# A fused two-block kernel: the last token tile's expert choice moved into the dense stage, other choices two heads at a time, 128-row expert biases

## The chip, the cores and the metric

The kernel runs as one program on one core of a Trainium2 chip. The metric is the device time of one launch in microseconds (us), as the median of several runs. The engines are named as in the profile: PE is TensorE's matmul side and PEld its weight loads, DVE is VectorE, ACT ScalarE, POOL GpSimd, SP SyncE.

## The reference, cut to what matters

Two transformer blocks over 512 tokens of 1024 numbers, all in float32. The first has a mixture of 32 experts with four chosen per token, the second a PEER layer: each of 8 heads picks 16 of 16384 small experts for every token.

```python
def moe_ffn(h, ...):
    top_logits, top_idx = lax.top_k(hf @ router_w + router_b, TOP_K)      # 4 of 32
    gates = jax.nn.softmax(top_logits, axis=-1)
    ...
        gu = xb @ w_gate_up[e] + b_gate_up[e]                             # 1024 -> 2048
        ...
        act = (up + 1.0) * gate * jax.nn.sigmoid(SWIGLU_ALPHA * gate)
        return act @ w_down[e] + b_down[e]                                # 1024 -> 1024
    ...
    out = out.at[tok_sorted].add(y_sorted * gate_sorted[:, None])

def _peer(h, w_query, sub_keys, expert_u, expert_v):
    q = (t @ w_query).reshape(n_tok, P_HEADS, 2, P_DQ)
    sc = jnp.einsum('thcd,hckd->thck', q, sub_keys)                       # 2 x 128 key scores per head
    s1, i1 = lax.top_k(sc[:, :, 0], 16); s2, i2 = lax.top_k(sc[:, :, 1], 16)
    cand = (s1[..., :, None] + s2[..., None, :]).reshape(n_tok, P_HEADS, 256)
    top_s, top_i = lax.top_k(cand, 16)
    experts = take(i1, top_i // 16) * 128 + take(i2, top_i % 16)
    gates = jax.nn.softmax(top_s, axis=-1)
    act = gelu(einsum('td,tkd->tk', t, expert_u[experts])) * gates
    return einsum('tk,tkd->td', act, expert_v[experts])
```

## The kernel before, in words

The program is written in one order; each engine works through its own queue in order when it runs. A planner in the framework chose the order of each queue when the kernel was built: it starts from the program's order as priorities and may put a later instruction ahead of an earlier one that waits. So work that stands late in the program can fill an earlier gap of an engine, as far as its data and its memory are there.

Large float32 products are taken as three products of two halves: `split` writes `hi`, a rounded copy (ACT, L116), and `lo`, the rest (DVE, L117, or POOL where asked), and PE multiplies hi by hi, hi by lo and lo by hi. Weights stream in over SP's queue, are split, and multiplied.

**The expert mixture (MoE).** `moe` (L660) goes over 32 experts of 96 token rows (CB) each. For expert i it issues the gate-up products (`Expert.gate_up`, L602), the next expert's token gather and its transposes (`load_x`, L578, `transpose_split`, L571), the down products of expert i-1 (`down`, L633), and the activation (`swiglu`). At odd i a piece of a side product runs (`ple`, L546 and L548), after i = 1 a piece of `slot_map`. Raw weights have four buffers (`wraw`), the halves three each. Four `gu` and two `dn` accumulators are opened by a bias product: `biases` (L641) lays each bias out as 64 rows, 32 of the rounded value and 32 of the rest; `sel` has for expert i ones in rows i and 32+i, so one matmul of 64 rows adds both halves to every token row (L672):

```python
bias = lambda t: (lambda out, n: nc.tensor.matmul(out, sel[:, i:i + 1].to_broadcast([64, CB]),
                                                  t[:, n * S:(n + 1) * S], start=True, stop=False))
```

There are four of these per expert for gate-up and two for down, 192 in all. The expert outputs are scattered to Y, and later gathered per token and weighted by the gates (`Route.rest`, L451, makes `e.gates`). Blocks beyond 96 rows of an expert go through an overflow loop with a bias of its own.

**The PEER layer**, in `peer` (L2084), has these stages. *Queries* (L1834): 16 half-heads c; the products give scores for 4 tiles of 128 tokens (NT); tiles 0 to 2 are searched at once (`best`, that is `top16`: five DVE operations for the best 16 of a row), and the scores of the last tile are kept in `sc3`. After each odd c the head's choice is made for three tiles (`select`, L1878): `pair_sums` adds 50 candidate pairs in seven small operations on DVE, and their numbers in seven on POOL (`cid`); `top16` for each tile; then `eq`, a mask of 16 x 50 on DVE (L1897), multiplied by `cid` on POOL (L1899), and summed on DVE a step later (`rest`, L1904). *Gates* (L1922): for tiles 0 to 2 the chosen experts become dense 128 x 128 gate tables by one-hot products (`ohA`, `ohB`, `gp`), written to DRAM (`GD`, L1959 to L1961); beside it the first 24 `up` products of the dense stage run (GEB). *The last tile's choice*, L2110 to L2117:

```python
for c in range(16):
    pr.best(pr.sel, pr.sc3[:, c], NT - 1, c)
rest = [pr.select(slice(NT - 1, NT), 0)]
for h in range(1, NH):
    rest.append(pr.select(slice(NT - 1, NT), h))
    rest.pop(0)()
```

*Dense stage*, 128 steps b: `up` streams 128 rows of expert_u for the three tiles (`up`, L1963, `dots`, then Gelu into `ge`, 24 steps ahead until it runs out), `acts` multiplies by the gates read back from `GD` (`gch`, one load for four steps, L1994; `dact` L1997, its halves `dah` and `dal`, L2003 and L2004), `down` adds the products with expert_v to `y` (L2012). Memory of the choice's pool is closed ahead of this stage and given to its tiles, `vhi` among them. Beside it, *gathers* (`gathered`, L2015): the last tile's experts aren't dense; in 144 turns POOL fetches one row of expert_u and one of expert_v per token (`gu`, `gv`, L2022), which DVE uses two turns later (L2032, L2043). A step takes one turn, two where b % 8 is 1 or 5. At b = 114 the gathers have to be through, and the last tile is finished.

The changed places in full:

Of the kernel before, what the change touches and what calls it, by code (L numbers as in the profile page):

```python
# [359 lines left out]
class Route:  # L360
# [90 lines left out]
    def rest(self):  # L451
# [10 lines left out]
        nc.vector.tensor_mul(e.gates, gt, gs.to_broadcast([P, NT, TOPK]))  # L462
        pe = pool.tile([P, NT, NE], F, name="pe")
# [91 lines left out]
class Expert:  # L555


    def __init__(self, e, pools, wgu, wdn, tok, out, bias_gu, bias_dn, nm):
        self.e, self.wgu, self.wdn, self.tok, self.out = e, wgu, wdn, tok, out
        self.bias_gu, self.bias_dn, self.nm = bias_gu, bias_dn, nm  # L560
        self.pw, self.px, self.ps_gu, self.ps_dn, self.ps_t = pools
        self.ahead = []
# [57 lines left out]
    def down(self):  # L620
# [20 lines left out]
def biases(e, pool, raw):  # L641

    nc, a = e.nc, e.a
    e.esel = e.mc.tile([64, NE], R, name="sel")
    for t_, nm in ((e.bg, "b_gate_up"), (e.bd, "b_down")):
        for o in range(0, t_.shape[1], D):
            r = raw([64, D], "braw")
            for h in range(2):
                nc.gpsimd.dma_start(r[32 * h:32 * h + 32, :], a[nm][:, o:o + D])
            t = t_[:, o:o + D]  # L650
            nc.scalar.copy(t, r)
            nc.vector.tensor_sub(t[32:64, :], r[32:64, :], t[32:64, :].bitcast(F))
# [6 lines left out]

def moe(e):  # L660
    nc, tc, a = e.nc, e.tc, e.a
    bg, bd, sel = e.bg, e.bd, e.esel
    with ExitStack() as c2:
# [7 lines left out]
        def make(i):  # L671
            bias = lambda t: (lambda out, n: nc.tensor.matmul(out, sel[:, i:i + 1].to_broadcast([64, CB]),  # L672
# [3 lines left out]
                          e.slot_tok[:, i:i + 1], e.slot_out[:, i:i + 1], bias(bg), bias(bd), str(i))  # L676
# [6 lines left out]
        side, smap = ple(e, px, ps_t), slot_map(e, px)  # L683
        for i, x in enumerate(ex):
# [29 lines left out]
        with tc.For_i(0, n_over, 1) as i:  # L714
# [7 lines left out]
            br2 = px.tile([P, D], F, name="ov_bd", bufs=1)  # L722
            nc.sync.dma_start(br2[0:1, :], a["b_down"][bass.ds(ei, 1), :])
# [6 lines left out]
                       so[:, 1:2], so[:, 0:1], bias(br), bias(br2), "o")  # L730
# [1045 lines left out]
class Peer:  # L1776
# [11 lines left out]
    def open(self, ctx):  # L1788
# [3 lines left out]
        self.s = self.pd.tile([P, NT, NH, 2, NK], F, name="pk_s")  # L1792
        self.ixu = self.pd.tile([P, NT, NH, 2, NK], U32, name="pk_iu")
# [4 lines left out]
        self.ts = self.sel.tile([P, NT, NH, NK], F, name="pk_ts", bufs=1)  # L1798
        self.idf = self.sel.tile([P, NT, NH, NK], F, name="pk_id", bufs=1)
# [34 lines left out]
    def queries(self, pool, ps, ahead):  # L1834
# [14 lines left out]
        for c in range(16):  # L1849
# [25 lines left out]
    def best(self, pool, sc, t, c):  # L1875
        top16(self.e, pool, sc, self.s[:, t, c // 2, c % 2, :], self.ixu[:, t, c // 2, c % 2, :], "a")

    def select(self, tiles, h):  # L1878

        e, nc, pool, s = self.e, self.e.nc, self.sel, self.s  # L1880
        n = tiles.stop - tiles.start
        ixf = pool.tile([P, NT - 1, 2, NK], F, name="pk_if")[:, 0:n]
        nc.vector.tensor_copy(ixf, self.ixu[:, tiles, h])
        cand = pool.tile([P, NT - 1, NC], F, name="cand")[:, 0:n]
        pair_sums(nc.vector, cand, s[:, tiles, h, 0, :], s[:, tiles, h, 1, :])
# [374 lines left out]
```

## Time and profile before

| what | value |
|---|---|
| median of 3 runs | 4267.72 us (4267.01 to 4272.81) |
| profiled execution | 4264.27 us, its span 4262.4 us |
| mean granted TensorE clock | 0.979 of full speed |
| PE, PEld | busy 4069.3 us (95%), 3240.0 us (76%) |
| DVE, ACT, POOL | busy 3162.1 us (74%), 2033.2 us (48%), 1047.8 us (25%) |

The span is the time from the first to the last instruction of the core in one profiled execution; the execution's own time has a little around it. A view of groups gives line, engine, operation, output and inputs by the program's names, shape and count, busy time and the mean of one in ns, and after the last bar the idle time ahead of it with what ended most of it. A timeline row is start, duration, engine, line, operation, shapes and count, and in brackets the idle time before it and its releaser. PEclk is the granted clock in tenths of full speed or as a share.

### The profile page before, as it was taken

The page shows a single profiled execution, that of the slowest core. Times are in us where ns is not written, and L with a number is a line of the kernel's source. Part 1 is how long each engine was busy: PE and PEld are TensorE (multiplying, and loading weights), DVE is VectorE, ACT ScalarE, POOL GpSimd, SP SyncE. Part 2 cuts the span into 40 slices and gives each one's busy share as a digit, 9 for nine tenths or more (in the row PEclk, how much of TensorE's full clock was granted, in tenths as well). Part 3 has the DMA queues.
Part 4 walks back from the last instruction along what each step waited for, and adds up shares of the span by engine and source line. Part 5 has one row for each costly group of instructions (what it writes and reads, how often), then busy time and mean ns, then how long its engine had stood idle before and what let it go on. Part 6 is the DMA issues. An engine that isn't in the chain of part 4 may idle for free. (4 is left out here: it accounts for less than half of the span.)

```text
span 4262.4 us, 60165 instructions
## 1 busy us (share of the span) xinstructions
PE 4069.3 (95%) x22534; PEld 3240.0 (76%) x22534; DVE 3162.1 (74%) x5533; ACT 2033.2 (48%) x2876; POOL 1047.8 (25%) x929
## 2 busy tenths in 40 slices
PE   9999999999999979999999999999896999999998
PEld 7556666666666638877888888777786999999997
DVE  8778888888888875766676666456988577777777
ACT  3356666666666654434444444333385333333333
POOL 5402221220000030110011110015556244344431
PEclk9999999999999989999999999999998999999999
DMA  3679999999999863212321222443155788888884
GB/s 126 212 292 330 334 348 330 335 346 334 338 342 332 333 225 98 73 63 83 95 85 58 77 75 78 148 135 109 65 193 207 263 300 308 311 310 302 304 303 166
DMA packets 355415, 933.84 MB, mean 219 GB/s; under 512 B 60928, under 2 KB 169376, under 8 KB 322224
## 3 DMA queue, kind: packets, MB, share of 16 engines
q1 hardware_dynamic: 299168, 741.19, 49.2%
q0 software_dynamic: 49536, 176.18, 11.2%
q10 hardware_dynamic: 6416, 12.58, 0.9%
q8 instruction: 179, 2.93, 0.3%
q14 instruction: 116, 0.95, 0.1%
HBM read 865.66 MB, written 64.20 MB: 218 GB/s over the span
## 5 line engine op out<-in xcount | busy, mean ns | idle before, releaser
L117 DVE TENSOR_TENSOR wlo<-wraw,whi 128x2048 fp32r<-128x2048 f32 x384 | 873.1, 2291 | 101.9 <-ACT whi L116 101.2
L116 ACT CAST whi<-wraw 128x2048 fp32r<-128x2048 f32 x384 | 721.5, 1909 | 124.6 <-DMA wraw<-in_w_gate_up_dram 88.4
L1972 PE MATMUL dots<-hp_h,ulo 128*128 128x384 f32 x1024 | 351.9, 344 | 15.6 <-POOL ulo L117 15.3
L1972 PE MATMUL dots<-hp_h,uhi 128*128 128x384 f32 x1024 | 352.7, 344 | 2.2 <-ACT uhi L116 2.2
L1972 PE MATMUL dots<-hp_l,uhi 128*128 128x384 f32 x1024 | 351.1, 343 | 0.0
L2022 POOL DMA_INDIRECT gu<-in_expert_u_dram,idx x128 | 193.5, 1512 | 432.3 <-DVE gu L2032 412.8
L602 PE MATMUL gu<-wlo,xhi 128*96 128x512 f32 x1024 | 297.5, 410 | 0.0
L602 PE MATMUL gu<-whi,xhi 128*96 128x512 f32 x1024 | 283.7, 397 | 0.6 <-ACT xhi L116 0.6
L116 ACT CAST uhi<-uraw 128x1024 fp32r<-128x1024 f32 x128 | 134.1, 1048 | 314.6 <-PE dots L1972 232.6
L602 PE MATMUL gu<-whi,xlo 128*96 128x512 f32 x1024 | 280.0, 394 | 0.0
L2012 PE MATMUL y<-vhi,dah 128*128 128x512 f32 x762 | 238.5, 394 | 28.8 <-ACT dah L2003 28.8
L2012 PE MATMUL y<-vhi,dal 128*128 128x512 f32 x762 | 236.3, 391 | 0.0
L2012 PE MATMUL y<-vlo,dah 128*128 128x512 f32 x762 | 235.8, 390 | 0.0
L602 PEld LDWEIGHTS gu<-whi,xhi 128*96 128x96 f32 x1024 | 163.2, 162 | 73.7 <-ACT yx L636 4.4
L602 PEld LDWEIGHTS gu<-whi,xlo 128*96 128x96 f32 x1024 | 165.4, 162 | 70.5
L2004 DVE TENSOR_TENSOR dal<-dact,dah 128x384 fp32r<-128x384 f32 x127 | 71.0, 559 | 197.5 <-ACT dah L2003 197.0
L2003 ACT CAST dah<-dact 128x384 fp32r<-128x384 f32 x127 | 65.1, 513 | 309.8 <-issue 261.1
L602 PEld LDWEIGHTS gu<-wlo,xhi 128*96 128x96 f32 x1024 | 158.8, 162 | 66.4 <-issue 8.9
L1972 PEld LDWEIGHTS dots<-hp_h,ulo 128*128 128x128 f32 x1024 | 194.9, 190 | 17.1 <-POOL ulo L117 16.3
L1972 PEld LDWEIGHTS dots<-hp_h,uhi 128*128 128x128 f32 x1024 | 195.0, 190 | 6.8 <-ACT uhi L116 2.6
L1972 PEld LDWEIGHTS dots<-hp_l,uhi 128*128 128x128 f32 x1024 | 195.1, 191 | 4.1
L578 POOL DMA_INDIRECT xg<-H,slot_tok x32 | 38.7, 1209 | 626.2 <-PE mtp L571 424.8
(720 smaller groups left out, 10397.7 us busy)
## 6 DMA issues: line engine op xcount, KB each, us to landing
wraw<-in_w_gate_up_dram SPq DMA_DIRECT2D x256, 1024.0 KB, 5.8
wraw<-in_w_down_dram SPq DMA_DIRECT2D x128, 1024.0 KB, 7.2
uraw<-in_uT_dram SPq DMA_DIRECT2D x128, 512.0 KB, 5.0
vraw<-in_expert_v_dram SPq DMA_DIRECT2D x128, 512.0 KB, 3.8
wuraw<-in_w2p_dram SPq DMA_DIRECT2D x72, 512.0 KB, 3.2
GD<-gst SPq DMA_DIRECT2D x36, 640.0 KB, 4.9
gch<-GD SPq DMA_DIRECT2D x30, 768.0 KB, 12.1
piece<-in_w_ada_dram SPq DMA_DIRECT2D x24, 512.0 KB, 4.1
```

What stands on the lines that cost most here:

```text
L116: e.copied = e.nc.scalar.copy(hi, src).ins
L117: (eng or e.nc.vector).tensor_sub(lo, src, hi.bitcast(F))
L578: e.gathered = nc.gpsimd.indirect_dma_start(out=xg, out_offset=None, in_=e.H, in_offset=bass.IndirectOffsetOnAxis(ap=self.tok, axis=0)).ins
L602: nc.tensor.matmul(self.gu[n], l[:, k, :], r[:, cs], start=False, stop=k == KD - 1 and r is lo)
L1972: nc.tensor.matmul(dots, l[:, k, :], r[:, k, 0:ND], start=k == 0 and i == 0, stop=k == KD - 1 and i == 2)
L2003: nc.scalar.copy(ah, act)
L2004: self.anchor = nc.vector.tensor_sub(al, act, ah.bitcast(F)).ins
L2012: self.e.nc.tensor.matmul(y[t][:, cs], l[:, t * P:(t + 1) * P], r[:, cs], start=b == 0 and l is ah and r is hi, stop=b == P - 1 and l is al)
L2022: nc.gpsimd.indirect_dma_start(out=g, out_offset=None, in_=src, in_offset=bass.IndirectOffsetOnAxis(ap=idx[:, h, k:k + 1], axis=0))
```

## The change

**Expert biases.** The gate-up bias and `sel` get 128 rows, of which rows 64 to 127 of the bias are zero. The down bias leaves the experts and the overflow loop: `Route.rest` spreads the gates over the 32 experts (`e.gm`), and a new generator `down_bias` transposes them (four transposes, one ACT copy) and adds gates times b_down to `e.xpre` by eight float32 matmuls of 32 rows and eight DVE additions, one after each even expert from i = 2 on.

```diff
+        e.gm = e.mc.tile([P, NT, NE], F, name="gm")
+        go = pool.tile([P, NT, TOPK, NE], F, name="go")
+        nc.vector.tensor_mul(go, oh, e.gates[:, :, :, None].to_broadcast([P, NT, TOPK, NE]))
+        nc.vector.reduce_sum(e.gm, go.rearrange("p t j e -> p t e j"), axis=AX.X)
...
-            self.bias_dn(dn[n], n)
         for k2 in range(4):
...
-    v = pool.tile([64, NE], F, name="selv", bufs=1)
+    e.esel = e.mc.tile([P, NE], R, name="sel")
+    nc.gpsimd.dma_start(e.bd, a["b_down"])
+    for o in range(0, 2 * D, D):
+        r = raw([P, D], "braw")
+        nc.gpsimd.memset(r[64:P, :], 0.0)
+        for h in range(2):
+            nc.gpsimd.dma_start(r[32 * h:32 * h + 32, :], a["b_gate_up"][:, o:o + D])
+        t = e.bg[:, o:o + D]
+        nc.scalar.copy(t, r)
+        nc.vector.tensor_sub(t[32:64, :], r[32:64, :], t[32:64, :].bitcast(F))
+    v = pool.tile([P, NE], F, name="selv", bufs=1)
...
+def down_bias(e, pool, ps):
+
+    nc = e.nc
+    gT = pool.tile([NE, S], F, name="gT", bufs=1)
+    t = ps.tile([P, S], F, name="gTp", tag="plep")[0:NE]
+    for i in range(NT):
+        nc.tensor.transpose(t[:, i * P:(i + 1) * P], e.gm[:, i, :], e.ident)
+    nc.scalar.copy(gT, t)
+    for i in range(NT):
+        for n in range(2):
+            yield
+            cs = slice(n * S, (n + 1) * S)
+            b = ps.tile([P, S], F, name="bdp", tag="plep")
+            nc.tensor.matmul(b, gT[:, i * P:(i + 1) * P], e.bd[:, cs], start=True, stop=True)
+            nc.vector.tensor_add(e.xpre[:, i, cs], e.xpre[:, i, cs], b)
+    yield
+
+
...
-            bias = lambda t: (lambda out, n: nc.tensor.matmul(out, sel[:, i:i + 1].to_broadcast([64, CB]),
+            bias = lambda t: (lambda out, n: nc.tensor.matmul(out, sel[:, i:i + 1].to_broadcast([P, CB]),
                                                               t[:, n * S:(n + 1) * S], start=True, stop=False))
...
             if i % 2 == 1:
                 next(side, None)
+            elif i > 1:
+                next(downs, None)
...
-                e.bg, e.bd = fp.tile([64, 2 * D], R, name="bg"), fp.tile([64, D], R, name="bd")
+                e.bg, e.bd = fp.tile([P, 2 * D], R, name="bg"), fp.tile([NE, D], F, name="bd")
```

**The choice for tiles 0 to 2.** The key scores and indices are kept in one tile for three token tiles and one for the last. `select` takes two heads, so six rows, at c = 3, 7, 11, 15, and the summing of a group follows two half-heads later, at c = 5, 9 and 13, and after the loop. `pairs` and `marked` are helpers shared with the last tile.

```diff
-        self.s = self.pd.tile([P, NT, NH, 2, NK], F, name="pk_s")
-        self.ixu = self.pd.tile([P, NT, NH, 2, NK], U32, name="pk_iu")
+        rows = lambda n, dt, nm: self.pd.tile([P, NH * n, 2, NK], dt, name=nm)
+        self.s, self.ixu = (rows(NT - 1, F, "pk_s"), rows(1, F, "pk_sl")), (rows(NT - 1, U32, "pk_iu"), rows(1, U32, "pk_il"))
...
-            if c % 2:
-                rest.append(self.select(slice(0, NT - 1), c // 2))
-            elif c:
+            if c % 4 == 3:
+                rest.append(self.select(c // 4))
+            elif c % 4 == 1 and c > 4:
                 rest.pop()()
...
+    def pairs(self, pool, last, rs):
...
+        nc.vector.tensor_copy(ixf, ixu[:, rs])
+        cand = pool.tile([P, n, NC], F, name="cand", bufs=1)
+        pair_sums(nc.vector, cand, s[:, rs, 0, :], s[:, rs, 1, :])
+        i1 = pool.tile([P, n, NK], F, name="i1")
         nc.vector.tensor_scalar(i1, ixf[:, :, 0, :], float(P), None, op0=OP.mult)
-        cid = pool.tile([P, NT - 1, NC], F, name="cid")[:, 0:n]
+        cid = pool.tile([P, n, NC], F, name="cid", bufs=1)
         pair_sums(nc.gpsimd, cid, i1, ixf[:, :, 1, :])
-        tu, tf = pool.tile([P, NT - 1, NK], U32, name="tu")[:, 0:n], pool.tile([P, NT - 1, NK], F, name="tf")[:, 0:n]
...
+        return cand, cid, pool.tile([P, n, NK], U32, name="tu"), pool.tile([P, n, NK], F, name="tf")
+
+    def marked(self, eq, io, tf, cid):
+        nc = self.e.nc
+        nc.vector.tensor_tensor(eq, io[:, None, 0:NC].to_broadcast([P, NK, NC]), tf[:, :, None].to_broadcast([P, NK, NC]),
+                                op=OP.is_equal)
+        nc.gpsimd.tensor_mul(eq, eq, cid[:, None, :].to_broadcast([P, NK, NC]))
+        return eq
...
+    def select(self, g):
...
+        e, nc, pool, n = self.e, self.e.nc, self.sel, NT - 1
+        cand, cid, tu, tf = self.pairs(pool, False, slice(2 * n * g, 2 * n * (g + 1)))
+        at = lambda x, r: x[:, r % n, 2 * g + r // n, :]
+        for r in range(2 * n):
+            top16(e, pool, cand[:, r, :], at(self.ts, r), tu[:, r, :], "b")
         nc.vector.tensor_copy(tf, tu)
...
+        eqs = [self.marked(pool.tile([P, NK, NC], F, name="eq", bufs=6), self.io_ps, tf[:, r, :], cid[:, r, :])
+               for r in range(2 * n)]
...
         def rest():
-            for t, eq in enumerate(eqs):
-                nc.vector.reduce_sum(self.idf[:, tiles.start + t, h, :], eq, axis=AX.X)
+            for r, eq in enumerate(eqs):
+                nc.vector.reduce_sum(at(self.idf, r), eq, axis=AX.X)
```

**The last tile's choice** becomes a generator, `late`, with its small tiles in the memory of `yg`, and masks in the gather buffers (`gt`). Eight dense steps take two `top16` rows each, then four groups of two heads take two steps each. The gathers follow at the same one `next` per dense step; the generator stops after two turns of every three, so of two steps one carries one gather turn and the other two.

```diff
+    def late(self, pool):
+
+        e, nc = self.e, self.e.nc
+        room, off, views = self.yg, [0], {}
...
+        ar = Arena()
+        ts, idf = ar.tile([P, NH, NK], F, name="l_ts"), ar.tile([P, NH, NK], F, name="l_id")
+        for c in range(0, 16, 2):
+            for i in range(2):
+                self.best(ar, self.sc3[:, c + i], NT - 1, c + i)
+            yield
+        for g in range(4):
+            cand, cid, tu, tf = self.pairs(ar, True, slice(2 * g, 2 * g + 2))
+            for i in range(2):
+                top16(e, ar, cand[:, i, :], ts[:, 2 * g + i, :], tu[:, i, :], "b")
+            nc.vector.tensor_copy(tf, tu)
+            yield
+            eqs = [self.marked(pool.tile([P, D], F, name="leq", tag="gt", bufs=6)[:, 0:NK * NC].rearrange("p (k c) -> p k c", k=NK),
+                               self.iota, tf[:, i, :], cid[:, i, :]) for i in range(2)]
+            yield
+            for i, eq in enumerate(eqs):
+                nc.vector.reduce_sum(idf[:, 2 * g + i, :], eq, axis=AX.X)
+        self.last_choice = self.chosen(ts, idf, self.pc, ar)
...
-    for c in range(16):
-        pr.best(pr.sel, pr.sc3[:, c], NT - 1, c)
-    rest = [pr.select(slice(NT - 1, NT), 0)]
-    for h in range(1, NH):
-        rest.append(pr.select(slice(NT - 1, NT), h))
-        rest.pop(0)()
-    rest.pop()()
-    idx, gt = pr.chosen(NT - 1, pr.pc)
...
-    gather = pr.gathered(idx, gt, pool)
+
+    def last_tile():
+        yield from pr.late(pool)
+        for i, x in enumerate(pr.gathered(*pr.last_choice, pool)):
+            if i % 3 < 2:
+                yield
+
+    gather = last_tile()
...
-        for _ in range(2 if b % 8 in (1, 5) else 1):
-            next(gather, None)
+        next(gather, None)
```

`chosen` takes its arrays and its pool as arguments, with the same operations as before.

## Rows read from the trace of the kernel before

**Rows 1.** The page's first part: busy time, share of the span, instructions of each engine

```profile
PE 4069.3 (95%) x22534; PEld 3240.0 (76%) x22534; DVE 3162.1 (74%) x5533; ACT 2033.2 (48%) x2876; POOL 1047.8 (25%) x929
```

**Rows 2.** Windows: us, busy PE, PEld, DVE, ACT, POOL (operations), PEclk, DMA, GB/s

```profile
228.00:1520.00 1292.00, 1279.86 (x5632) 867.54 (x5632) 1088.77 (x806) 841.21 (x660) 192.30 (x94) 1.00 0.91 334
...
3040.00:3077.00 37.00, 21.68 (x90) 20.96 (x90) 31.77 (x127) 11.61 (x16) 18.52 (x16) 0.72 0.28 100
3077.00:3258.00 181.00, 169.25 (x1192) 159.00 (x1190) 154.47 (x375) 145.72 (x331) 113.71 (x127) 1.00 0.51 189
3258.00:3287.00 29.00, 0.23 (x2) 0.00 (x0) 27.56 (x70) 6.10 (x8) 18.06 (x37) 0.54 0.34 106
...
3680.00:3810.00 130.00, 130.00 (x654) 118.38 (x654) 98.77 (x122) 45.21 (x63) 54.44 (x40) 1.00 0.85 306
```

**Rows 3.** Timeline of PE around an expert's down bias (start us, us, operation)

```profile
664.72 0.62 PE L602 MATMUL gu<-wlo,xhi 128*96 128x512 f32 x2
665.18 0.49 PE L571 MATMUL mtp<-ident,sw_a 96*128 96x96 f32 x4
...
666.91 1.09 PE L602 MATMUL gu<-whi,xlo 128*96 128x512 f32 x4
667.93 0.46 PE L672 MATMUL dn<-bd,sel 64*96 64x512 f32 x1
668.33 1.18 PE L602 MATMUL gu<-wlo,xhi 128*96 128x512 f32 x4
```

**Rows 4.** Windows, tile sel alone: us, busy PE, PEld, DVE, then as before

```profile
228.00:1520.00 1292.00, 80.23 (x192) 28.17 (x192) 0.00 (x0) 1.00 0.91 334
```

**Rows 5.** Waits of ACT, 400 to 1400 us: total us, times, longest

```profile
ACT whi L116 <- DMA wraw<-in_w_gate_up_dram: 79.9, 46, 4.1
```

**Rows 6.** Windows: ten microseconds of the MoE, columns as in Rows 2

```profile
610.00:620.00 10.00, 10.00 (x43) 6.22 (x41) 9.01 (x9) 3.32 (x4) 0.00 (x0) 1.00 1.05 384
```

**Rows 7.** Timelines of SP, ACT, DVE and PE at the hand-over to the dense stage

```profile
3253.77 1.86 SPq L1961 DMA_DIRECT2D GD<-gst  x3
...
3280.57 1.04 ACT L116 CAST vhi<-vraw 128x1024 fp32r<-128x1024 f32 x1 [3.67 <-POOL eq L1899]
3280.72 1.19 ACTq L1994 DMA_DIRECT2D gch<-GD  x2
...
3285.86 1.03 DVE L1997 TENSOR_TENSOR dact<-ge,gch 128x384 f32<-128x384 f32 x2 [0.61 <-DMA gch<-GD]
...
3287.02 1.22 PE L2012 MATMUL y<-vhi,dah 128*128 128x512 f32 x2 [28.79 <-ACT dah L2003]
```

**Rows 8.** DMA issues: queue, count, KB of one, median us from issue to landing

```profile
GD<-gst SPq DMA_DIRECT2D x36, 640.0 KB, 4.9
```

**Rows 9.** Timeline of DVE in a dense step with two gather turns

```profile
3711.32 0.56 DVE L2004 TENSOR_TENSOR dal<-dact,dah 128x384 fp32r<-128x384 f32 x1 [2.09 <-ACT dah L2003]
...
3715.28 1.22 DVE L2032 SCALAR_TENSOR_TENSOR gu<-gu,hp_g 128x1024 f32<-128x1024 f32 x1
...
3716.42 1.28 DVE L2043 SCALAR_TENSOR_TENSOR yg<-gv,pact,yg 128x1024 f32<-128x1024 f32 x1
...
3719.67 0.56 DVE L2004 TENSOR_TENSOR dal<-dact,dah 128x384 fp32r<-128x384 f32 x1 [0.34 <-ACT dah L2003]
```

**Rows 10.** Tile gu, 3500 to 3900 us: issue ns min/median/max, then landing

```profile
L2022 POOL DMA_INDIRECT gu<-in_expert_u_dram,idx x60: 933/1678/1687, 3504.3 to 3897.2; - x60
...
DMA to landing us min/median/max: 5.6/6.6/9.7
```

**Rows 11.** Timeline of PE: float32 matmuls of 256 columns

```profile
689.51 1.56 PE L546 MATMUL plep<-wg,hT 128*128 128x256 f32 x6
```

**Rows 12.** Timeline of DVE where the routing ends

```profile
203.71 0.19 DVE L418 SCALAR_TENSOR_TENSOR q<-pp,selt 128x32 f32<-128x32 f32 x1 [7.62 <-PE pp L417]
```

**Rows 13.** Groups by form of POOL, 2900 to 3070 us

```profile
L1899 POOL TENSOR_TENSOR eq<-eq,cid 128x800 f32<-128x800 f32 x24 | 41.5, 1756 | 17.0 <-DVE eq L1897 17.0
```

**Rows 14.** Timeline of PE at the end of the queries

```profile
3046.77 0.69 PE L1972 MATMUL dots<-hp_h,ulo 128*128 128x384 f32 x1 [6.71 <-POOL ulo L117]
```

**Rows 15.** Windows, tile pk_s alone: us, DVE busy, PEclk, DMA, GB/s

```profile
3077.00:3258.00 181.00, 27.06 (x135) 1.00 0.51 189
```

More of the change, by code (lines that the diff above doesn't have):

```diff
@@ L633, in down @@
                         nc.tensor.matmul(dn[n], l[:, k, :], r[:, j * D + n * S:j * D + (n + 1) * S],
-                                         start=False, stop=k == KD - 1 and r is lo)
+                                         start=k == 0 and l is ah and r is hi, stop=k == KD - 1 and r is lo)
         for n in range(2):
@@ L643, in biases @@
     nc, a = e.nc, e.a
[L644 to L652, printed above, removed]
-    v = pool.tile([64, NE], F, name="selv", bufs=1)
+    e.esel = e.mc.tile([P, NE], R, name="sel")
[9 more added lines that the diff above has]
+    v = pool.tile([P, NE], F, name="selv", bufs=1)
     nc.gpsimd.iota(v, pattern=[[1, NE]], base=0, channel_multiplier=-1, allow_small_or_imprecise_dtypes=True)
-    v2 = pool.tile([64, NE], F, name="selv2", bufs=1)
+    v2 = pool.tile([P, NE], F, name="selv2", bufs=1)
     nc.vector.tensor_scalar(v2, v, -32.0, None, op0=OP.is_equal)
     nc.vector.scalar_tensor_tensor(e.esel, v, 0.0, v2, op0=OP.is_equal, op1=OP.add)
+def down_bias(e, pool, ps):
[13 more added lines that the diff above has]
+    yield
 def moe(e):
     nc, tc, a = e.nc, e.tc, e.a
-    bg, bd, sel = e.bg, e.bd, e.esel
+    bg, sel = e.bg, e.esel
     with ExitStack() as c2:
@@ L696, in moe @@
         prev.down()
-        for it in (side, smap):
+        for it in (side, smap, downs):
             for _ in it:
@@ L1875, in best @@
     def best(self, pool, sc, t, c):
[L1876 to L1885, printed above, removed]
-        i1 = pool.tile([P, NT - 1, NK], F, name="i1")[:, 0:n]
+        last = t == NT - 1
@@ new lines, in best @@
+        r = c // 2 if last else c // 2 * (NT - 1) + t
+        top16(self.e, pool, sc, self.s[last][:, r, c % 2, :], self.ixu[last][:, r, c % 2, :], "a")
+    def pairs(self, pool, last, rs):
+        nc, n = self.e.nc, rs.stop - rs.start
+        s, ixu = self.s[last], self.ixu[last]
+        ixf = pool.tile([P, n, 2, NK], F, name="pk_if")
+        nc.vector.tensor_copy(ixf, ixu[:, rs])
+        cand = pool.tile([P, n, NC], F, name="cand", bufs=1)
+        pair_sums(nc.vector, cand, s[:, rs, 0, :], s[:, rs, 1, :])
+        i1 = pool.tile([P, n, NK], F, name="i1")
@@ L1887, in select @@
         nc.vector.tensor_scalar(i1, ixf[:, :, 0, :], float(P), None, op0=OP.mult)
-        cid = pool.tile([P, NT - 1, NC], F, name="cid")[:, 0:n]
+        cid = pool.tile([P, n, NC], F, name="cid", bufs=1)
         pair_sums(nc.gpsimd, cid, i1, ixf[:, :, 1, :])
-        tu, tf = pool.tile([P, NT - 1, NK], U32, name="tu")[:, 0:n], pool.tile([P, NT - 1, NK], F, name="tf")[:, 0:n]
-        for t in range(n):
-            top16(e, pool, cand[:, t, :], self.ts[:, tiles.start + t, h, :], tu[:, t, :], "b")
@@ L1893, in select @@
-        nc.vector.tensor_copy(tf, tu)
-        eqs = []
-        for t in range(n):
-            eq = pool.tile([P, NK, NC], F, name="eq", bufs=6)
-            nc.vector.tensor_tensor(eq, self.io_ps[:, None, 0:NC].to_broadcast([P, NK, NC]),
-                                    tf[:, t, :, None].to_broadcast([P, NK, NC]), op=OP.is_equal)
-            nc.gpsimd.tensor_mul(eq, eq, cid[:, t:t + 1, :].to_broadcast([P, NK, NC]))
-            eqs.append(eq)
+        return cand, cid, pool.tile([P, n, NK], U32, name="tu"), pool.tile([P, n, NK], F, name="tf")
```

37 lines of the change are left out of this document (23 added, 14 removed).

## The prediction, written before the change was run

> **What bounds the kernel now.** I read five views, from coarse to fine. The busy share of each engine [rows 1]: TensorE (PE) is busy 95% of the span, so a change pays only where it takes PE work away or fills a PE gap. Busy time by stage [rows 2]: the stages touched differ. In the MoE (228 to 1520) PE idles 12 of 1292 us, with the DMA engines 0.91 busy. Around the choice of experts PE idles 15.3 of 37, then 11.8 of 181, then 28.8 of 29 us. In the dense stage it never idles, and the vector engine (DVE) is 76% busy. Third, the PE timeline of one expert bias [rows 3, 4] shows what PE is busy with. Fourth, the waits of the MoE [rows 5, 6] tell what would bind next. Last, the hand-over into the dense stage [rows 7, 8], where the longest gap lies, and a dense step [rows 9, 10], which has to take the moved work.
>
> **Expert biases (MoE).** In a run, matmuls follow one another every 0.232 us: two started at 664.72 and the next operation at 665.18, and four take 1.09 where two take 0.62, so 0.23 by the one and 0.235 by the other. The 64-row bias breaks the run: the free slot after 666.91 is 667.84, the bias starts at 667.93, its successor at 668.33, and that group takes 1.18 where others take 1.09. That is 0.09 + 0.40 + 0.09 = 0.58 us for one matmul, 0.35 above the pace [rows 3]. How many visits: the 192 bias matmuls cover 80.2 us [rows 4]; with 0.46 for a visit of one and 0.232 for each further matmul, 80.2 = 192 x 0.232 + V x 0.23, so V = 155; I take 150. Removed: the 64 down biases, 64 x 0.232 = 15 us, and, with all rows of the array in use in the other 128, the excess of 150 visits, 53 us. Bounds of the excess: zero if rows are not its cause, 192 x 0.35 = 67 if each bias goes alone.
>
> Added is down_bias: eight float32 matmuls of 32 rows x 512 columns. The nearest row is a float32 matmul of 256 columns, two records each, six records in 1.56 us, so 0.23 a record [rows 11]; 512 columns are four, 0.93 us, and with 0.35 for a visit 1.3. Eight are 10 us, the transposes 1: 11 us. Lower bound 8 x 0.232 = 2, upper 20 if a 32-row visit costs twice a 64-row one. Its eight DVE additions (0.75 us each, by the 0.56 for 384 columns [rows 9]) lie in the 203 us that DVE idles here [rows 2]; without that cover they would cost 6 us. Net PE work removed: 68 - 11 = 57 us.
>
> How much arrives? 57 us over 32 experts is 1.8 us each. The weight stream must then run at 334 x 1292/1235 = 349 GB/s; ten microseconds reached 384 [rows 6]. The scalar engine (ACT), which splits the weights first, waited 80 us for weights between 400 and 1400 [rows 5]; if PE is faster, that wait grows. I take three quarters, **43 us** (15 to 60).
>
> Ahead of the MoE, two DVE operations of 512 elements for e.gm are added, 1.5 us; they fit into a DVE idle of 7.6 us [rows 12]. One bias chunk of three is no longer split, two memsets on GpSimd (POOL) are new: nothing, or 2 us if POOL delays the first token gather.
>
> **Two heads together (queries).** Four groups instead of eight save 4 x 10 small DVE operations, 0.1 us each (half of 27.06/135, as such operations overlap [rows 15]): 4 us, and some of the last tile's rows leave this stage too. DVE is busy 32 of 37 us at its end, so this counts. Against it, the last group sends six products of 1.76 us to POOL in one go instead of three [rows 13], and PE already waits there for POOL's ulo, queued behind such products [rows 14]: up to 5 us back. I take **4 us** (-5 to +10).
>
> **The gates stage** loses the last tile's DVE work, by tile pk_s alone 27 of 154 us [rows 15]. PE idles 11.8 us there, for products that DVE feeds late; ACT, busy 146 of 181 us, stays [rows 2]. I take **7 us** (0 to 12).
>
> **The hand-over.** PE stands 28.8 us for the first dah [rows 7]. The chain: the last eq product on POOL, then vhi (it waits for that memory), the gch loads behind it on ACT's queue at 3280.7, dact at 3285.9. All before gch can go. Next late is the gates' own output: GD's last writes are issued by 3255.6 and land in 4.9 us [rows 8], 3260.5; gch takes 5.1, dact and dah 1.1: PE starts at 3266.8 instead of 3287.0. If gch needs only the first, small write, it is 3262. I take **21 us** (15 to 25).
>
> **The dense stage** takes the choice in 16 steps without gathers. On DVE that choice now costs about 27 us in the gates [rows 15], 27 at the hand-over [rows 2] and a few before, some 59, or 3.7 us a step, where a step carries 1.25 gather turns of two operations, 1.22 and 1.28 us [rows 9], 3.1. On POOL each of four groups adds seven small sums and two products; only the first gathers stand behind them, which could not start earlier. DVE's reduction waits for products issued one step before. ACT takes one Exp with its table loads where it is 35% busy; SP's queue is passed by nothing. But the 144 gather turns now fall on steps 16 to 112, three in two steps: half of the steps carry two turns, where a quarter does now. Such a step exists [rows 9]: 3711.3 to 3719.7, 8.35 us, with 0.34 us of DVE idle left, and PE runs through at 8.33 us a step. The mean DVE load goes from 6.33 to 6.33 + 0.25 x 2.5 = 7.0 us. Bytes per step grow from 2.55 MB (306 GB/s x 8.33) by 0.25 x 1.05, so the rate becomes 338 GB/s and the DMA share 0.94. A gather lands in 6.6 us, at most 9.7 [rows 10], and has two steps. I cost all this at **2 us** (0 to 20).
>
> **A page that speaks against it.** By rows 3 PE works at 0.232 us for 512 columns between the biases, so I count its busy time as a bound; weight loads are busy 67% of the MoE [rows 2]. The Trainium skill (Trainium Kernel Development and Optimization, Performance Expectations) says that matmul busy time tells little of how near a kernel is to its limit, and that the share of weight loads is a better measure. By it PE would have slack in the MoE, which would give nothing, and the sum would be 30 us; that is rival (a) taken to its end.
>
> **The sum** is 43 + 4 + 7 + 21 - 2 = 73 us. The profiled execution took 4264.3 us (span 4262.4 and 1.9 around it), 3.4 below the median of 4267.7; so 4191 for it and 4195 for a median.
>
> **Rivals.**
> (a) *The weight stream becomes the MoE's bound.* For it: 0.91 of the DMA time is used, ACT waits 80 us for weights, only four raw buffers run ahead. Against: 384 GB/s was reached. The MoE then gives 15 us, in all 45: 4223.
> (b) *Rows are not the cause of the bias gap*; it could be the one broadcast column as the stationary operand. Against: 96-row transposes join the same stream at 665.18, without a gap [rows 3]. Then only the down biases' share remains, 15 + 50 x 0.35 - 11 = 21, three quarters of it 16, in all 46: 4222.
> (c) *The choice is planned back ahead of the dense stage, or POOL's six products take the place of the waits removed*: for queries and gates the change doesn't do what it says. 11 us less: 4206.
> (d) *The dense step overflows; slower.* The place is DVE. It idles 31 of 130 us, 2.0 a step; with 0.34 in a double step a single one has (2.0 - 0.25 x 0.34)/0.75 = 2.55. If that much stayed in each step, a step would take 7.0 + 2.55 = 9.55 us; the point from which it decides is 8.33. 88 steps x 1.2 = 106 us, in all 33 slower: 4301. Against: the wait for dah does shrink, 2.09 to 0.34 between neighbours [rows 9].
> (e) *Gathers starve.* An issue takes POOL 1.68 us [rows 10], three of them 5.0 of 8.33, beside DVE at 76%. If each also waits out a DVE operation of 1.25 us, POOL needs 8.8 us a step: 88 x 0.47 = 41 us back, 4236. The Trainium skill (SBUF — State Buffer, SBUF: two separate sides) has this rule: GpSimd and DVE operations with two inputs take a shared port in turns, the loser blocked for a whole instruction. Issues of 0.93 us stand beside those of 1.68 [rows 10], so part of it may be in the price already.
>
> **How the numbers follow.** The forecast 0.55, (a) 0.17, (b) 0.07, (c) 0.10, (d) 0.06, (e) 0.05. About 0.2%, 8.5 us, is what a measurement of this kernel can tell from no change. All but (d) are faster by more than that; of (a) and (e) at their worst 0.02 falls within it: 0.92, 0.02, 0.06. The forecast's own range is 4172 to 4214 (MoE 25 to 58, hand-over 15 to 25). To leave out no more than 2 in 10 it takes in (a) to (c) with their spread, and nearly the full MoE gain together with the hand-over's: 4160 to 4234.
>
> **What would show it.** In the changed profile: no down biases in the expert stream, gate-up biases as 128*96 at 0.232 us; the MoE near 1249 us, with more waits for wraw; PE's waits for ulo at the queries' end no longer than 15 us; the wait for the first dah 4 to 10 us instead of 28.8; dense steps of 8.33 us with PE at 100% and DVE near 83%. The forecast is wrong if the MoE stays above 1270 us, if PE idles over 10 us in the dense stage, or if the hand-over still waits for an eq product.

## The result and the profile after

The changed kernel takes **4211.94 us** (median of 4 runs, 4209.88 to 4213.16) against 4267.36 before: ratio 0.9875, 95% interval 0.986 to 0.989, 55 us less. Its profiled execution took 4213.16 us with a span of 4211.4, 51.0 less than the span before.

Where the 51 us come from is read from windows cut at landmarks: the first and last expert product, query product, gate product and `y` product of each trace. First the kernel before, then the changed one; the columns are those of [rows 2].

```profile
0.00:232.60 232.60, 210.07 (x960) 144.76 (x960) 174.17 (x329) 79.11 (x100) 105.99 (x106) 0.96 0.47 159
232.60:1519.20 1286.60, 1275.74 (x5622) 865.40 (x5622) 1084.35 (x803) 838.55 (x657) 192.30 (x94) 1.00 0.91 335
...
3033.90:3078.70 44.80, 29.45 (x134) 27.92 (x133) 39.56 (x182) 14.93 (x24) 21.43 (x25) 0.77 0.29 104
3078.70:3252.50 173.80, 162.05 (x1151) 152.07 (x1151) 149.16 (x364) 142.38 (x324) 107.49 (x110) 1.00 0.50 186
3252.50:3287.00 34.50, 5.73 (x34) 5.40 (x32) 31.18 (x78) 7.74 (x10) 22.70 (x52) 0.61 0.39 132
3287.00:4248.40 961.40, 961.38 (x4763) 867.16 (x4764) 705.45 (x904) 336.40 (x476) 350.08 (x254) 1.00 0.81 290
```

```profile
0.00:238.30 238.30, 209.17 (x961) 144.72 (x961) 174.28 (x330) 78.64 (x100) 107.48 (x107) 0.96 0.46 155
238.30:1489.60 1251.30, 1233.75 (x5576) 861.08 (x5576) 1086.30 (x807) 838.64 (x656) 281.36 (x94) 1.00 0.94 345
...
3003.20:3043.60 40.40, 28.23 (x136) 26.51 (x135) 39.01 (x183) 13.13 (x25) 19.57 (x18) 0.83 0.30 104
3043.60:3208.10 164.50, 159.88 (x1139) 149.39 (x1138) 118.76 (x177) 141.58 (x321) 102.47 (x93) 1.00 0.50 191
3208.10:3227.10 19.00, 7.68 (x45) 7.35 (x43) 11.40 (x38) 6.07 (x8) 0.00 (x0) 0.80 0.89 325
3227.10:4197.00 969.90, 964.94 (x4762) 869.89 (x4763) 742.69 (x1080) 337.46 (x478) 380.15 (x292) 0.99 0.80 286
```

Row by row: the start of the MoE comes 5.7 us later, the MoE is 35.3 shorter, the queries' end 4.4, the gates 9.3, the hand-over 15.5, and the dense stage is 8.5 longer. The rest differs by under 1.

**The biases** are what the diff promised. PE's timeline of the changed kernel (compare [rows 3]):

```profile
643.92 1.09 PE L606 MATMUL gu<-whi,xlo 128*96 128x512 f32 x4
644.93 1.12 PE L677 MATMUL bdp<-bd,gT 32*128 32x512 f32 x2
645.99 1.17 PE L606 MATMUL gu<-wlo,xhi 128*96 128x512 f32 x4
647.00 0.62 PE L635 MATMUL dn<-whi,ahi 128*96 128x512 f32 x2
...
651.97 0.63 PE L694 MATMUL gu<-bg,sel 128*96 128x512 f32 x2
652.44 0.60 PE L550 MATMUL plep<-wg,hT 128*128 128x256 f32 x2
```

Two 128-row biases start their successor 0.47 us later, 0.235 each, the pace of the stream. The 32-row `bdp` breaks it, as the 64-row ones did: 1.06 us to its successor and 0.08 on either side, 1.2 in all.

**Ahead of the MoE** something new waits. ACT in the changed kernel, then PE:

```profile
231.93 0.57 ACT L671 COPY gT<-gTp 32x512 f32<-32x512 f32 x1 [6.92 <-PE gTp L670]
232.41 5.49 ACT L116 CAST whi<-wraw 128x2048 fp32r<-128x2048 f32 x3
```

```profile
238.33 2.02 PE L606 MATMUL gu<-whi,xhi 128*96 128x512 f32 x4 [5.84 <-ACT xhi L116]
```

The planner put `down_bias`'s only ACT copy, gT, ahead of the first expert's casts. It waits 6.9 us for PE's transposes, and the casts queue behind it.

**The hand-over**, the rows that answer to [rows 7], from SP, ACT, DVE and PE (SPq and ACTq are DMA issues on that engine's queue):

```profile
3209.38 1.91 SPq L2031 DMA_DIRECT2D GD<-gst  x3
...
3215.64 1.04 ACT L116 CAST uhi<-uraw 128x1024 fp32r<-128x1024 f32 x1 [3.19 <-PE dots L2042]
3215.73 1.75 ACTq L2064 DMA_DIRECT2D gch<-GD  x2
...
3219.29 3.48 DVE L117 TENSOR_TENSOR vlo<-vraw,vhi 128x1024 fp32r<-128x1024 f32 x3
...
3225.72 0.28 DVE L1793 MATCH_REPLACE8 yg<-pk_sl,sc 128x128 f32<-128x128 f32 x1
3225.91 1.03 DVE L2067 TENSOR_TENSOR dact<-ge,gch 128x384 f32<-128x384 f32 x2
...
3227.12 1.22 PE L2082 MATMUL y<-vhi,dah 128*128 128x512 f32 x2 [11.34 <-ACT dah L2073]
```

PE's wait fell from 28.8 to 11.3 us. No product on POOL stands in the chain any more; what is late is `gch`, issued behind a cast that waits for PE. The view of that one load gives its time to landing:

```profile
DMA to landing us min/median/max: 6.7/6.7/6.7
```

So it landed at 3222.5, 6.7 us after its issue; in the kernel before it was 4.9. `dact` started 3.4 us later still, and not because it waited for the load: DVE was at work without a gap, on `vlo` until 3222.8 and then on rows of the last tile's choice (the last of them is shown) that the planner had put ahead of it.

**The dense stage** lost its time in its first 62 us. DVE, ACT and PE there:

```profile
3286.93 0.98 DVE L1975 TENSOR_REDUCE yg<-leq 128x16 f32<-128x800 f32 x1 [0.71 <-POOL leq L1921]
...
3288.60 1.22 DVE L117 TENSOR_TENSOR ulo<-uraw,uhi 128x1024 fp32r<-128x1024 f32 x1
...
3268.71 1.28 ACT L1985 ACT_TABLE_LOAD   x1
3281.61 0.31 ACT L1985 ACTIVATE pgt<-pgt 128x128 f32<-128x128 f32 x1 [11.62 <-DVE pgt L1984]
...
3283.62 1.04 ACT L116 CAST uhi<-uraw 128x1024 fp32r<-128x1024 f32 x1
...
3289.88 0.69 PE L2042 MATMUL dots<-hp_h,ulo 128*128 128x384 f32 x1 [4.54 <-DVE ulo L117]
```

The choice, written over sixteen steps, was through by 3288, in the eighth: the planner pulled it forward. DVE then waits for POOL's masks with `ulo` queued behind; on ACT the softmax's Exp waits 11.6 us for DVE with `ge` and `uhi` queued behind. PE waits 0.4 and 4.5 us, and runs the five microseconds after its restart at a mean granted clock of 0.52, so nearly all of them at the lower of the two levels, 1.2 of 2.4 GHz:

```profile
3289.88:3294.88 5.00, 5.00 (x16) 5.00 (x17) 4.97 (x7) 0.00 (x0) 4.05 (x4) 0.52 0.87 288
```

In the whole stage PE idles 5.0 us and is busy 3.6 us longer than before. Later everything is as forecast:

```profile
3626.00:3759.00 133.00, 133.00 (x670) 121.31 (x669) 109.35 (x138) 46.88 (x66) 66.00 (x48) 1.00 0.94 338
```

PE never idle, DVE 82% busy, 0.94 and 338 GB/s.

### The profile page after: what moved, and what is told of

It reads as the page before. It is cut to its first block, busy times and chain, and to the rows that moved or that the text cites. A ratio compares the mean times of both kernels' runs of the same rounds, so it can differ in the third digit from the quotient of the medians.

```text
span 4211.4 us, 59952 instructions
## 1 busy us (share of the span) xinstructions
PE 4024.9 (96%) x22490; PEld 3237.1 (77%) x22490; DVE 3148.2 (75%) x5462; ACT 2031.0 (48%) x2874; POOL 1137.9 (27%) x874
## 3 DMA queue, kind: packets, MB, share of 16 engines
q0 software_dynamic: 49488, 176.05, 11.3%
## 5 line engine op out<-in xcount | busy, mean ns | idle before, releaser
L2092 POOL DMA_INDIRECT gu<-in_expert_u_dram,idx x128 | 182.2, 1423 | 370.6 <-DVE gu L2102 356.5
L2082 PE MATMUL y<-vhi,dah 128*128 128x512 f32 x762 | 239.0, 395 | 11.3 <-ACT dah L2073 11.3
L2082 PE MATMUL y<-vlo,dah 128*128 128x512 f32 x762 | 236.0, 391 | 0.0
L117 DVE TENSOR_TENSOR ulo<-uraw,uhi 128x1024 fp32r<-128x1024 f32 x121 | 154.2, 1275 | 71.7 <-ACT uhi L116 71.7
L2092 POOL DMA_INDIRECT gv<-in_expert_v_dram,idx x128 | 172.9, 1351 | 107.2 <-DVE yg L2113 73.3
L639 POOL DMA_INDIRECT Y<-yx,slot_out x32 | 105.8, 3306 | 353.8 <-ACT yx L638 353.0
```

The costliest lines, as they stand in the source:

```text
L117: (eng or e.nc.vector).tensor_sub(lo, src, hi.bitcast(F))
L639: nc.gpsimd.indirect_dma_start(out=e.Y, out_offset=bass.IndirectOffsetOnAxis(ap=self.out, axis=0), in_=y, in_offset=None)
L2082: self.e.nc.tensor.matmul(y[t][:, cs], l[:, t * P:(t + 1) * P], r[:, cs], start=b == 0 and l is ah and r is hi, stop=b == P - 1 and l is al)
L2092: nc.gpsimd.indirect_dma_start(out=g, out_offset=None, in_=src, in_offset=bass.IndirectOffsetOnAxis(ap=idx[:, h, k:k + 1], axis=0))
```

## The experiments

Stages in us, between the same landmarks (queries' end: last query product to first gate product):

| kernel | median | to MoE | MoE | queries' end | gates | hand-over | dense |
|---|---|---|---|---|---|---|---|
| before | 4267.4 | 232.6 | 1286.6 | 44.8 | 173.8 | 34.5 | 961.4 |
| changed | 4211.9 | 238.3 | 1251.3 | 40.4 | 164.5 | 19.0 | 969.9 |
| e1_bias_only | 4234.1 | 236.0 | 1252.0 | 44.8 | 174.3 | 34.6 | 961.1 |
| e2_rows64 | 4236.3 | 238.6 | 1275.1 | 39.9 | 164.5 | 19.0 | 969.6 |
| e3_peer_only | 4242.1 | 231.7 | 1286.4 | 39.8 | 164.6 | 19.0 | 969.6 |
| e4_gT_later | 4205.4 | 235.4 | 1250.1 | 40.3 | 164.9 | 19.0 | 969.7 |
| e5_paced | 4199.1 | 235.4 | 1252.8 | 37.2 | 164.4 | 16.7 | 961.8 |
| e6_one_head | 4213.6 | 239.5 | 1250.3 | 44.0 | 165.2 | 17.1 | 970.0 |
| e7_turns2 | 4214.5 | 237.8 | 1251.1 | 40.4 | 164.6 | 19.0 | 969.9 |
| e8_gch_first | 4212.0 | 237.9 | 1252.3 | 39.9 | 162.4 | 13.1 | 977.2 |
| e9_both | 4190.1 | 230.4 | 1250.6 | 37.0 | 164.4 | 16.6 | 961.8 |
| e10_no_gu_bias | 4197.1 | 235.7 | 1240.2 | 40.3 | 164.9 | 19.0 | 969.8 |
| e12_gd_early | 4208.1 | 237.8 | 1254.0 | 40.4 | 162.3 | 9.0 | 976.5 |

The start of the MoE scatters by some 4 us between profiled executions; the stages that an edit doesn't touch repeat within 1.5, the MoE within 4.

**One half of the change at a time (e1_bias_only, e3_peer_only).** The diff is applied to the kernel before, split at the PEER functions.

> The kernel before with the bias part of the change alone (128-row gate-up biases, down biases moved to down_bias), the choice of experts as before. Theory (the parts simply add, as the two traces show them by stage): the expert stage 35 us shorter, its start 6 us later, so 4267 - 35 + 6 - 1 = 4237 us (4232 to 4243). Rival (the planner trades one part against the other, or what the expert stage gains is lost where the second block begins): under 15 us of gain, 4252 or more.

> The kernel before with the choice of experts changed alone (two heads at a time, the last tile's choice in the dense stage), biases as before. Theory (the parts add by stage): queries 4.4, gates 9.3 and hand-over 15.5 us shorter, the dense stage 8.6 longer, so 4267 - 20.6 = 4247 us (4242 to 4251). Rival (the choice moved gives nothing by itself, its stages only shift with the rest): 4262 or more.

Measured 4234.1 (ratio 0.9932, 0.9919 to 0.9945) and 4242.1 (0.9947, 0.9934 to 0.9959). Against 4265.7 for the kernel before, measured with them, that is 31.6 and 23.6 us, 55.2 together: the halves add, and each gain stands in its own stages.

**64 rows again (e2_rows64).**

```diff
-sel[:, i:i + 1].to_broadcast([P, CB])
+sel[:, i:i + 1].to_broadcast([64, CB])
```

and 64 rows for `bg`, `sel` and their sources.

> The changed kernel with 64-row gate-up biases again (bias and selector of 64 rows; the down biases stay out of the experts). Theory (the number of rows sets what a bias costs between the experts' products): the bias matmuls go back from 0.28 to 0.37 us each and their neighbours slow down again, 128 x 0.09 plus some 10 us around them, about 20 us: 4232 us (4224 to 4245), with the gate-up bias at 0.40 us to its successor. Rival (rows do not matter, the down biases were all of the gain): 4212, the bias at 0.235 us.

```profile
668.93 0.62 PE L635 MATMUL dn<-wlo,ahi 128*96 128x512 f32 x2
669.48 0.46 PE L693 MATMUL gu<-bg,sel 64*96 64x512 f32 x1
669.88 1.16 PE L606 MATMUL gu<-whi,xhi 128*96 128x512 f32 x4
670.88 1.08 PE L606 MATMUL gu<-whi,xlo 128*96 128x512 f32 x4
```

4236.3 (ratio 0.993, 0.9918 to 0.9943): the MoE is 1275.1, and the bias takes 0.40 us to its successor again. Of the 35.3 us the rows give 23.8 and the down biases' move 11.5. Rival (b) falls. The Trainium skill (TensorE: Matmul & The Clock Gate, Why this matters for your kernels) says that a lone matmul of 32 rows takes as long as one of 128. In this stream 64 rows and 128 don't: 0.40 against 0.235 us from one start to the next, and the measurement decides.

**The gT copy (e4_gT_later).**

```diff
-    nc.scalar.copy(gT, t)
+    with e.tc.issue_after(e.copied):
+        nc.scalar.copy(gT, t)
```

> The changed kernel with the copy of the transposed gates (gT) queued on ACT behind a cast of expert 2 instead of ahead of the first expert's casts. Theory (that copy waited 6.9 us for PE at the head of ACT's queue and held the first three casts back, so the expert stage began 5.7 us later): 4212 - 5.7 = 4206 us (4204 to 4209), the first gate-up product at about 232.5 us instead of 238.3. Rival (the stage is paced by the weights anyway, so a later start is made up): 4212, with the stage as much longer as it starts earlier.

4205.4 (ratio 0.9859, 0.9844 to 0.9873). The wait of the first expert product fell from 5.84 to 0.61 us:

```profile
235.36 2.02 PE L606 MATMUL gu<-whi,xhi 128*96 128x512 f32 x4 [0.61 <-ACT xhi L116]
```

The 2.9 us in the table are less because that execution reached ACT's copy of `ada`, just ahead, 2.0 us later. By the medians 6.5 us are gained, but the runs of the two kernels overlap (4203.1 to 4212.7 against 4209.9 to 4213.2). The same edit on top of e5's shows it clear of the noise: e9_both is 9.0 us below e5_paced (4186.3 to 4193.6 against 4196.7 to 4201.6).

**The choice at its written pace (e5_paced).**

```diff
-        yield from pr.late(pool)
+        late = pr.late(pool)
+        while True:
+            with tc.issue_after(pr.anchor):
+                if next(late, late) is late:
+                    break
+            yield
```

> The changed kernel with every part of the last tile's choice queued on DVE behind the dense step it is written in (after that step's dal), so that the planner cannot pull it forward. Theory (in the changed kernel the sixteen parts run in some seven steps, DVE is full there, ulo and the Exp on ACT come late, PE idles 4.9 us and then runs at the lower clock): the dense stage goes from 969.9 to about 962 us, 4212 - 8 = 4204 us (4201 to 4208), no wait of PE for ulo. Rival (the dense stage is longer because it has more to do, however it is spread): 969 or more, 4212 or more.

4199.1 (ratio 0.9852, 0.9835 to 0.9869), better than expected: the dense stage is back at 961.8 with no wait of PE in it, and the choice no longer begins in the queries. The tile's view in the changed kernel has the first best-of-8 of all 16 of its rows there, from 2898 to 3022 us, and in this one from 3219 on:

```profile
L1791 DVE MAX8 pk_sl<-sc x16: 273/278/285, 2898.2 to 3022.3; 128x8 f32<-128x128 f32 x16
```

```profile
L1791 DVE MAX8 pk_sl<-sc x16: 275/281/290, 3219.0 to 3259.4; 128x8 f32<-128x128 f32 x16
```

That gives 3.2 us at the queries' end and 2.3 at the hand-over. How the work was spread, and not its amount, cost the dense stage 8.1 of its 8.5 us.

**One head at a time (e6_one_head).** `select` takes three rows after every odd c, as before.

> The changed kernel with the choice for tiles 0 to 2 taken one head at a time again, eight groups of three rows; the last tile's choice stays in the dense stage. Theory (two heads together give the queries' end its 4.4 us, by fewer small operations): queries to first gate product 44 instead of 40.4 us, 4212 + 4 = 4216 us (4213 to 4219). Rival (what helped there is that the last tile's rows left the stage): 40 us, 4212. Third (POOL's six products in one go cost time): shorter than 40, 4208.

4213.6 (ratio 0.9886, 0.9869 to 0.9903): the queries' end is 44.0 again, the number of the theory. Its reason, fewer small operations, isn't what the waits show. PE's wait there for POOL's `ulo`, in the kernel before and in the changed one:

```profile
PE dots L1972 <- POOL ulo L117: 15.3, 3, 6.7
```

```profile
PE dots L2042 <- POOL ulo L117: 3.4, 1, 3.4
```

With one head at a time it is 12.1 us again, and 3.7 more for ACT's `uhi`; with pairs PE waits 7.5 us for DVE's `ef` instead. The hand-over gives 1.9 back. So the pairs are worth 3.6 us in their stage, and 1.7 in all, which these runs don't tell from nothing.

**Fuller dense steps (e7_turns2).**

```diff
-            if i % 3 < 2:
+            if i % 2:
```

> The changed kernel with two gather turns in every dense step that has any (72 steps instead of 96), so that every such step is as full as the fullest now. By the rows of the changed kernel DVE then needs 6.85 + 0.5 x 2.5 = 8.1 us of 8.33, and the DMA engines 0.94 x (338 + 63)/338 = 1.1. Theory (a step keeps 8.33 us as long as DVE does, and the DMA share is the limit that ends it): the steps stretch by the DMA's excess, to 8.33 x 1.05 to 1.15, 30 to 90 us over 72 steps, 4240 to 4300. Rival (room is left on both, as the turns wait where they must): 4212, PE at 100%.

```profile
3626.00:3759.00 133.00, 133.00 (x670) 121.28 (x669) 126.39 (x161) 46.56 (x66) 90.24 (x65) 1.00 1.04 398
```

My theory missed: with two turns in each of 72 steps DVE is 95% busy, the DMA engines count as 1.04, and PE is busy in all 133 us. 4214.5 (ratio 0.9886, 0.9868 to 0.9903). So rivals (d) and (e) had no ground in a steady step.

**The first gates (e8_gch_first, e12_gd_early).** e8 issues every `gch` on SP and queues four `uraw` loads behind the first; e12 also leaves the last chunk's large gate writes out and writes the chunk before it twice instead (that edit isn't shown).

```diff
-            (nc.scalar if b < GB0 else nc.sync).dma_start(self.g, ...)
+            self.gload = nc.sync.dma_start(self.g, ...).ins
...
+            with tc.issue_after(pr.gload) if b < 4 else nullcontext():
+                ge[b + GEB] = pr.up(b + GEB)
```

> The changed kernel with the first gate loads (gch) on SP's queue, and the next four loads of uraw in the loop queued behind them. Theory (gch waited on ACT's queue behind two uhi casts that wait for PE, until 3215.7 us, though the gates it needs had landed by 3211, and then shared the DMA engines with uraw and vraw): it starts 3 to 4 us and lands 5 to 8 us earlier, PE's wait for the first dah falls from 11.3 to 3 to 6 us, 4212 - 6 = 4206 us (4203 to 4209). Rival (SP's queue is held up by earlier loads that wait for their buffers): no better than now, 4211 or more.

> The kernel with gch first on SP's queue, and in place of the last chunk's large gate writes (GD, three of 640 KB) the chunk before is written twice, so that nothing large stands ahead of the first gch (the dense gates of 32 tokens are then those of their neighbours from row 8 on). Theory (gch lands late since it shares the DMA engines with these writes): it lands 5 us after its issue instead of 8.6, the first y product comes 3 to 4 us earlier than in that kernel, 13.1 to 9.5 us behind the last gate product, gates, hand-over and dense together 1149 instead of 1152.7. Rival (its own many small packets or the uraw loads behind it take that long): 8 us or more again, 13 us.

The issue and the first use in e8, and then in e12:

```profile
3209.68 1.20 SPq L2064 DMA_DIRECT2D gch<-GD  x1
...
3218.25 0.56 DVE L2067 TENSOR_TENSOR dact<-ge,gch 128x384 f32<-128x384 f32 x1 [6.14 <-DMA gch<-GD]
```

```profile
3208.14 0.37 SPq L2066 DMA_DIRECT2D gch<-GD  x1
...
3213.34 0.56 DVE L2069 TENSOR_TENSOR dact<-ge,gch 128x384 f32<-128x384 f32 x1 [2.08 <-DMA gch<-GD]
```

With three writes of 640 KB just ahead of it the load is used 8.6 us after its issue, without them 5.2: here the writes hold it up, as the theory of e12 said. In the changed kernel they don't: its last write landed at 3215.6, before `gch` was issued. But e8 gains nothing (4212.0, ratio 0.988, 0.9863 to 0.9896; PE waits 12.5 us for dah): its `uraw` loads wait too, so PE runs out of up products sooner (busy 0.6 us in the hand-over instead of 7.7) and has them to do later, in the dense stage. e12 took 4208.1 (ratio 0.9865, 0.9849 to 0.9881), and gates, hand-over and dense together 1147.8 against 1152.7 in e8 and 1153.4 in the changed kernel. A kernel that keeps these writes and issues them behind `gch` wasn't tried.

**What bounds the MoE now (e10_no_gu_bias).**

```diff
-        for n in range(4):
-            self.bias_gu(self.gu[n], n)
```

> The changed kernel without the gate-up biases of the 32 experts (they are left out; the first product opens the accumulator), to see what bounds the expert stage of 1251 us now. Theory (PE's busy time bounds it, its products at 0.232 us): 128 matmuls of 0.28 us fall away, 36 us; at three quarters, as much as arrived of the change's own saving, the stage takes 1222 us (1215 to 1230), in all 4184. Rival (the stream of weights bounds it, DMA at 0.94): the stage stays at 1245 or more, in all 4205 or more, with PE idle 30 us longer.

PE's waits in the MoE, in the changed kernel and then in this one (us in total, times, longest):

```profile
PE dn L635 <- DVE wlo L117: 13.0, 21, 1.4
```

```profile
PE dn L633 <- DVE wlo L117: 27.1, 35, 1.4
```

Between the two theories: 4197.1 (ratio 0.984, 0.9826 to 0.9853), the MoE 1240.2, so 11 of 36 us arrive and PE's wait for split weights doubles. What is behind that wait, the stream itself or the two splits, this run doesn't tell apart. Against the stream alone speaks that ACT's own wait for raw weights in the MoE was 110.0 us in the changed kernel and is 89.7 here (96.6 before).

**Both corrections (e9_both).** The edits of e4 and e5 together.

> The changed kernel with both corrections: the gT copy behind expert 2's cast, and every part of the last tile's choice behind the dense step it is written in. Theory (the two losses stand in different stages and add): 4212 - 6 - 12 = 4194 us (4190 to 4198), with 0.6 us of wait at the first gate-up product and no wait of PE in the dense stage. Rival (they overlap, or the planner takes one back): 4199 or more, as with the pacing alone.

4190.1 us (ratio 0.9822, 0.9808 to 0.9835): the gains of e4 and e5 add, and this version beats the kernel before by 77 us and the changed one by 22.

## Why the prediction was right, and where its terms were off

The forecast was 4195 in a range of 4160 to 4234; 4211.9 lies in it, and inside the forecast's own 4172 to 4214. The main mechanisms held; of 73 us, 51 (profiled executions) to 55 (medians) came. Two terms were right by number and not by their reason, and are marked so.

- **Bias visits: the price held, the time that came free was less.** "0.35 above the pace" for 150 visits: in the trace of the kernel before there are 145, and from the product ahead to the product behind a visit costs 0.345 us above the pace where a bias stands alone between 512-column products (40 of them) and 0.335 where two stand together (16); ahead of `ple`'s products it is the same, and behind transposes 0.32 more than in the same place of the changed kernel. With the down biases that makes about 64 us, and some 53 after what down_bias costs, an estimate from these rows (57 was forecast). PE's busy time fell by only 42 us (1275.7 to 1233.8). A part of the missing 11 is short waits that count as busy: a product's record lasts 0.39 us where the next one can start after 0.235. Here is one in the changed kernel, on DVE and PE:

```profile
572.32 2.28 DVE L117 TENSOR_TENSOR wlo<-wraw,whi 128x2048 fp32r<-128x2048 f32 x1
...
574.29 0.40 PE L694 MATMUL gu<-bg,sel 128*96 128x512 f32 x1
574.65 0.70 PE L635 MATMUL dn<-wlo,ahi 128*96 128x512 f32 x2
```

  The product behind this bias starts 0.36 us after it and not 0.235, 0.05 us after `wlo` ended. Behind the 43 lone biases between such products it is 0.13 us more than the pace on average, 5.6 in all; the rest of the 11 isn't accounted for. The price of down_bias (11 us) was right by luck: eight visits of 1.2 us, but each as two records of 0.53 us, not four of 0.23 and 0.35 on top.
- **Three quarters arrive: too many.** Of these 53 us, 35.3 arrived, two thirds; 35.3 is 84% of the 42 by which PE's recorded busy time fell. e2 shows much the same for the rows alone: 115 visits at 0.34 are 39 us, and 23.8 came. As far as the waits show, PE then stands for split weights (7.5 us for DVE's `wlo` before, 13.0 after), and e10 has this grow to 27.1: of the next 36 us, 11 come. Rival (a) placed such a limit at 15 us and named the weight stream; whether it is the stream stays open. The rule of the Trainium skill that was weighed there (Trainium Kernel Development and Optimization, Performance Expectations) would have had the MoE give nothing; the trace disagrees by 35 us.
- **Ahead of the MoE: a term left out.** The prediction priced down_bias on PE and DVE and left out its one copy on ACT, gT. Not the copy itself (0.57 us) but the queue behind it pays: the MoE starts 5.7 us later.
- **Two heads 4: right by number, in part by luck. Gates 7: right.** Measured 4.4 and 9.3. The 4 us were to come from DVE's small operations, with PE's wait for POOL's `ulo` as a cost of up to 5. That wait fell instead, from 15.3 to 3.4 us, a new one of 7.5 for DVE came, and the choice that ran there too early took 3.2 back (e5). Of the 9.3, PE's idle time gave 7.1; 2 us of up products moved behind the last gate product.
- **The hand-over: the second chain mis-sized.** It gave 15.5 us of 21, and PE's wait is 11.3 instead of the 4 to 10 forecast. By the prediction's chain the first `y` product comes 14.3 us after the last gate product, and it came 19.0 after. "gch takes 5.1" became 6.7 to its landing, and then `dact` stood 3.4 us behind other work on DVE's queue, most of it the choice that was to run later. The prediction has no term for that. With the choice paced (e5) `dact` does wait for `gch`, 4.2 us, and 2.3 us come back.
- **The dense stage: "16 steps" failed.** A steady step is as predicted (8.33 us, DVE 82 for 83%, 338 GB/s). But the prediction let the choice keep its written pace and cost the Exp on ACT at nothing, without asking what is queued behind it. The planner ran it in eight steps and the stage is 8.5 us longer, not 2; e5 shows the pace alone to be worth 8.1 of them. Of rival (c), "planned back", there was a part: the first operations of the sixteen rows already ran in the queries, 3.2 us of their end (e5). The prices of (d) and (e) count 88 steps where the text has gathers in 96 (16 to 112); neither came true.

## What to carry to other kernels

Price a helper operation by what it does to the queue that it joins: one small copy with a late input, put ahead of ready work, cost 5.7 us here, and one ordering edge took the wait away. In a stream of 128-row matmuls, try padding a short contraction with zero rows: here that gave 23.8 us, and taking the down biases out 11.5. Spreading work over steps in the source spreads it in time only if something ties each part to its step.

## What the runs showed of the hardware that was not expected

- POOL's mask product takes 1.72 to 1.78 us in the queries and up to 3.48 in the dense stage. Beside it DVE's operations stretch. Two rows of the changed kernel, POOL's product from 3239.99 to 3241.74 and this one in it:

```profile
3239.99 1.75 POOL L1921 TENSOR_TENSOR leq<-leq,yg 128x800 f32<-128x800 f32 x1 [0.99 <-DVE leq L1919]
```

```profile
3240.04 2.11 DVE L2074 TENSOR_TENSOR dal<-dact,dah 128x384 fp32r<-128x384 f32 x1
```

  The same operation takes 0.55 elsewhere: it ended 0.4 us after POOL's. The Trainium skill (SBUF — State Buffer, SBUF: two separate sides) has the rule that these engines take a shared port in turns for a whole instruction; this row agrees.
- A DMA share of 1.03 at 397 GB/s over 400 us (e7, 3500 to 3900) left PE busy in all of them.
- After 4.5 us without work PE's mean granted clock over the next five was 0.52 (3289.88 to 3294.88), lower than the 0.59 over the first five after the 28.8 us gap of the kernel before.
- A wait of PE can hide in its busy time: a 512-column record lasts 0.39 us where the next can start after 0.235, so a wait of up to some 0.16 us, an estimate from these two numbers, shows only in the starts (574.29 to 574.65 above).
